# Hybrid decoder trunk in float32: one split of a weight block for both halves of the sequence, with the second half's products parked in DRAM

## The chip, the cores and the metric

The kernel runs on one core of a Trainium2 chip. The metric is device time in microseconds: the median of the runs shown, and beside it one profiled execution with its trace. In the views, PE is TensorE (matrix products), PEld its weight loads, DVE is VectorE, ACT is ScalarE, POOL is GpSimd and SP is SyncE, from whose queue most transfers are issued.

## The reference

Two layers act on a sequence of 1024 rows of width 1024, in float32. Layer 0 is the hybrid mixer; the change lies in its input projection. Cut to that part:

```python
proj = x @ w_in
qa, ka, va, qkv_b, z, beta_logit, a_logit = split_cols(proj, HYB_SPLITS)
o_a = sliding_window_attention(rope(qa), rope(ka), va, sinks)        # 8 heads of 64, window 128
qkv_b = silu(causal_dwconv(qkv_b, conv_w))                           # width 4, over rows
qb, kb, vb = split_cols(qkv_b, (B_W, B_W, B_W))                      # 4 heads of 128
o_b = gated_delta_rule(l2_normalize(qb), l2_normalize(kb), vb, g, beta)
o_b = rms_norm(o_b) * norm_w * silu(z)
mix = concatenate([o_a, o_b]) @ w_out
x = layer_norm(alpha * x + mix)
x = layer_norm(alpha * x + sqrelu_mlp(x))                            # 1024 -> 4096 -> 1024
```

Layer 1 has a gated linear recurrence in the mixer's place, and the same MLP.

## The kernel before

**Two chunks.** The sequence is cut into two chunks of 512 rows, `c` = 0 and 1. Each is a Python generator, `stream(c)`: hybrid mixer, output projection and layer norm (`mix_out`), MLP and layer norm (`mlp_ln`), then the same for layer 1. Chunk 1 needs from chunk 0 the last three rows of each convolution (`halo`), the delta states (`Sst`) and the previous keys and values of the attention.

**Products.** Every float32 operand of a large product is split in two parts of a shorter format, `h` (a cast) and `l` (the rest, by subtraction). `mm3` makes one product from three matmuls (h x h, h x l, l x h). `wblock` loads a weight block of 128x1024 into `ws` (three buffers), and `split` casts it into `wh` on ACT (each fifth one on VectorE) and subtracts into `wl` on VectorE or GpSimd (two buffers each). `proj_fm` projects a block of 128 output features: 8 steps of `mm3`, 24 matmuls of 128x512, into one PSUM bank of the four called `mm`. The four banks called `mx` take the small products. All matmuls are issued at line 206, transposes at line 210, and all other instructions at line 178, a wrapper.

**The hybrid stage.** `hybrid(c)` makes k, v and the two logits (`kv_proj`, 4 blocks of 264 columns), the queries of the attention (`q_proj`, 4 blocks), and per delta head four blocks by `proj_fm`: k, q, v in `head_front` (convolution, then silu into a tile of a ring) and z in `head_z`. `head_mid` is a head's scan: a chain of small products on PE with VectorE and ACT between, its last part four steps over the state `S`. Chunk 0 takes its tiles from two rings by turns, `t` (11 tiles, heads 0 and 2) and `s` (10 tiles, heads 1 and 3), and so has two scans under way; chunk 1 has `t` alone and one scan. A scan holds 8 tiles of its ring, of which three come from `head_front`. The ring `f` (4 tiles) holds rows for convolutions and for z. A ring's tile is asked for with `need(ring, n)`, which blocks the generator until n are free. Large tiles `g` (14) hold activations: a chunk's x takes four.

**What sets the order.** PE's order is written by the program: a main loop steps the generators, and a planner (`Clock`) keeps an estimate of every engine's time. Scans, attention, layer norms and loads of x run as `mixers`, which go first whenever the planner thinks their inputs ready; otherwise the loop takes the next step of a stream, streams in an earlier `phase` first, chunk 0 before chunk 1. A stream that is blocked gives way to the other. The order on the other queues, SP among them, is set by the framework's scheduler from the dependencies.

**The MLP.** `mlp` works in groups of 512 hidden features. `straight` makes a group with 4 + 4 blocks. `seven` makes a pair of groups' second product with seven block products in place of eight; it uses sums of weight blocks that are built in DRAM (`t1` to `t4`, loads `ws<-t`). Chunk 0 goes over from `straight` to pairs at an even group, once chunk 1's output projection is done (`"op"`) and two `g` tiles are free.

Of the kernel before, what the change touches and what calls it, by code (L numbers as in the profile page):

```python
# [9 lines left out]
F32 = mybir.dt.float32  # L10
# [7 lines left out]
P = 128  # L18
D = 1024
T = 1024  # L20
CH = 512
NT = CH // P
KT = D // P
# [190 lines left out]
def trunk(ctx: ExitStack, tc, I, out):  # L214
    nc = tc.nc
    clk = Clock(tc, nc)
    V, G, S, PE = clk.engine(nc.vector, "V"), clk.engine(nc.gpsimd, "G"), clk.engine(nc.scalar, "S"), clk
    DS, DA, DG = clk.engine(nc.sync, "V"), clk.engine(nc.scalar, "V"), clk.engine(nc.gpsimd, "V")
# [9 lines left out]
    dpool = ctx.enter_context(tc.tile_pool(name="dpool", bufs=1, space=bass.MemoryType.DRAM))  # L228
# [23 lines left out]
    def tl(r, dt=F32):  # L252
        return take(r, tpool.tile([P, FW if r == "f" else 512], dt, tag=r, name=nm(r), bufs=RINGS[r]))

    def ts(r, dt=F32):
        return tl(r, dt)[:, :512]

    def free(r, *tiles):
        rings[r] += len(tiles)
        spare[r] += [t.name for t in tiles]  # L260
        assert rings[r] <= (GB if r == "g" else RINGS[r])

    def need(r, n=1):
        return wait(lambda: rings[r] >= n)
# [4 lines left out]
    def wait(cond):  # L269
        while not cond():  # L270
            yield BLOCK
# [77 lines left out]
    def wblock(src, n=1024, hl=None, pool=True):  # L349
        st = clk.tile("ws", WS, wpool.tile([P, 1024], F32, tag="ws", name=nm("ws"), bufs=WS))[:, :n]  # L350
        DS.dma_start(st if len(src.shape) == 2 else st.rearrange("p (q c) -> p q c", q=2), src)
        if hl is None:
            hl = [clk.tile(t, WB, wpool.tile([P, 1024], F32R, tag=t, name=nm(t), bufs=WB))[:, :n] for t in ("wh", "wl")]
        h, l = hl
        split(h, l, st, pool and wcount[0] % LG)
        m = n // 2
        return [h[:, :m], h[:, m:]], [l[:, :m], l[:, m:]]

    def mm3(ps, lh, ll, rh, rl, start, stop, more=False):

        PE.matmul(ps, lh, rh, start=start, stop=False, fresh=more)
        PE.matmul(ps, lh, rl, start=False, stop=False, fresh=more)
        PE.matmul(ps, ll, rh, start=False, stop=stop, fresh=more)
# [34 lines left out]
    def load_xT(c, x, k2):  # L398
        if c == 0:
            st = [ts("t") for _ in range(2)]  # L400
            for j in range(2):
                DS.dma_start(st[j], I["xT"][:, 2 * k2 + j, :CH])
            free("t", *st)
        else:
            st = clk.tile("ws", WS, wpool.tile([P, 1024], F32, tag="ws", name=nm("ws"), bufs=WS))[:, :1024]
            DS.dma_start(st.rearrange("p (k t) -> p k t", k=2), I["xT"][:, 2 * k2:2 * k2 + 2, CH:])
            st = [st[:, :512], st[:, 512:]]
        for j in range(2):
            k = 2 * k2 + j
            S.copy(x.h(k), st[j])  # L410
            V.tensor_tensor(x.l(k), st[j], x.h(k), ALU.subtract)

    def proj_fm(src, x, bank=None, pool=True):
        wh, wl = wblock(src, pool=pool)
        ps = (bank or mm_ps)()
        for k in range(KT):
            b, c = divmod(k, 4)
            mm3(ps, wh[b][:, c * P:(c + 1) * P], wl[b][:, c * P:(c + 1) * P], x.h(k), x.l(k), k == 0, k == KT - 1)
            if k < KT - 1:
                yield  # L420
        return ps

    def proj_tm(srcs, x, n, nk=KT, pre=None, pool=True):
        ps = [mm_ps() for _ in range(NT)]
# [335 lines left out]
    def q_proj(c, x, st, oT):  # L760
        ps = yield from proj_tm([I["hin_q"][i] for i in range(4)], x, 512)
        st["q"] = [oT.quad(0, n) for n in range(NT)]
        for n in range(NT):
            split_ps(*st["q"][n], v4(ps[n]))
        yield UNIT
# [140 lines left out]
    def conv4(raw, y, tmp, wt, bias=None, pool=True):  # L906
        if bias is None:
            S.activation(y, raw[:, 0:512], AF.Copy, scale=wt(0))
        else:
            S.activation(y, raw[:, 0:512], AF.Identity, bias=bias, scale=wt(0))  # L910
        S.activation(tmp, raw[:, 1:513], AF.Copy, scale=wt(1))
        (G if pool else V).tensor_tensor(y, y, tmp, ALU.add)
        for j in range(2, 4):
            V.scalar_tensor_tensor(y, raw[:, j:j + 512], wt(j), y, ALU.mult, ALU.add)

    def head_front(c, h, x, d, r):
        for j, name in enumerate("kqv"):
            yield from need(r, 1)
            yield from need("f", 2)
            raw, y, u = tl("f"), ts("f"), ts(r)  # L920
            ps = yield from proj_fm(I["hin_fm"][h * 4 + j], x)
            i = h * 3 + j
            if c == 0:
                G.memset(raw[:, 0:3], 0.0)
            else:
                G.tensor_copy(raw[:, 0:3], halo[:, i, :])
            S.copy(raw[:, 3:515], ps)
            if c == 0:
                G.tensor_copy(halo[:, i, :], raw[:, 512:515])
            conv4(raw, y, u, lambda k: W["hcw"][:, i * 4 + k:i * 4 + k + 1])  # L930
            S.activation(u, y, AF.Tanh, scale=0.5)
            V.scalar_tensor_tensor(u, u, 1.0, y, ALU.add, ALU.mult)
            free("f", raw, y)
            d[name] = u
            yield UNIT

    def head_z(h, x, oT, d):
        yield from need("f")
        z = ts("f")
        ps = yield from proj_fm(I["hin_fm"][h * 4 + 3], x)  # L940
        S.activation(z, ps, AF.Tanh, scale=0.5)
        V.scalar_tensor_tensor(z, z, 1.0, ps, ALU.add, ALU.mult)
        S.copy(oT.h(4 + h), z)
        V.tensor_tensor(oT.l(4 + h), z, oT.h(4 + h), ALU.subtract)
        free("f", z)
        d["z"] = True
        yield UNIT

# [265 lines left out]
    def spawn(g, t=0.0):  # L1214
        mixers.append([lambda: t, g])

    def slots(n):
        slot["g"] = [gran() for _ in range(n // 4)]
        return [g[:, i * 512:(i + 1) * 512] for g in slot["g"] for i in range(4)]
# [20 lines left out]
    def load_x(c, x):  # L1240
        yield from need("g", 4)
        x.claim()
        for k2 in range(KT // 2):
            load_xT(c, x, k2)
            t = clk.now + 7.0
            yield lambda: t
        st[c]["x"] = True

    def hybrid(c, x, oT, st, rs):
        d = [dict() for _ in range(4)]  # L1250
        if c == 0:
            slot["tl"] = slots(8)
            yield from kv_proj(c, x, st, oT, lambda k2: load_xT(c, x, k2))
            DS.dma_start(csb, I["consts"])
        else:
            yield from wait(lambda: "x" in st)
            yield from head_front(c, 0, x, d[0], rs[0])
            yield from wait(lambda: sts[0].get("att", 0) >= 2)
            yield from kv_proj(c, x, st, oT, None)
        spawn(delta_scalars(c, st))  # L1260

        def q():
            yield from need("g", 2)
            yield from q_proj(c, x, st, oT)
            o = [dict() for _ in range(NT)]
            spawn(attention(c, st, oT, o))
            spawn(attn_preps(c, st, o))
        par = len(rs) > 1
        if not par:
            yield from q()  # L1270
        for h in range(4):
            if h or par:
                yield from head_front(c, h, x, d[h], rs[h % len(rs)])
            if not par and h:
                if h == 1:
                    yield from wait(lambda: "ln0" in sts[0])
                    yield from need("g", 2)
                yield from head_z(h - 1, x, oT, d[h - 1])
            yield from wait(lambda: h - st.get("scan", 0) < len(rs))
            spawn(head_mid(c, h, st, d[h], oT, rs[h % len(rs)]))  # L1280
            if h == 1 and par:
                yield from q()
                yield from need("g", 2)
                yield from head_z(0, x, oT, d[0])
                yield from head_z(1, x, oT, d[1])
                spawn(load_x(1, xTs[1]))
        if par:
            yield from head_z(2, x, oT, d[2])
        yield from head_z(3, x, oT, d[3])
        x.free()  # L1290
        yield from wait(lambda: st.get("mids") == 4 and st.get("att") == 4)

    def mix_out(w, oT, resid, which, r, s, t, hold):
# [34 lines left out]
    sts = st  # L1328

    xTs = [ActT(), ActT()]  # L1330
# [30 lines left out]
    while streams or mixers:  # L1361
        m = next((m for m in mixers if m[0]() + MARGIN <= clk.now), None) if clk.bank("mx", 4) <= clk.now else None
        if m is not None:
            r = next(m[1], "end")
# [11 lines left out]
        for c in ([cur] if cur is not None else sorted(streams, key=lambda c: (c == shy, phase[c], c))):  # L1376
            r = next(streams[c], "end")
# [129 lines left out]
```

## Time and profile before

| what | value |
|---|---|
| median of 3 runs | 2313.34 us (2312.12 to 2314.28) |
| profiled execution, its own time | 2313.61 us |
| its span, first to last instruction | 2311.8 us |
| PE busy | 2226.8 us, 96% of the span |
| VectorE, ACT, GpSimd busy | 1552.7, 1026.1, 313.6 us |
| loads of 512 KB of `hin_fm` (the blocks of `proj_fm` in the hybrid stage) | 32 |
| loads of 512 KB of sums for `seven` | 88 |
| mean granted clock of PE | 0.988 |

The profile's page gives busy time per engine, the span in 40 slices, the DMA queues, the chain of work that ended last and the costliest groups of instructions. A group's row has the line, the engine, the operation, output<-inputs, shapes and count; then busy time, mean nanoseconds of one, and the idle time of the engine just before with what ended it. A busy PE is not always a fast one: matmuls are pipelined, and the clock that it is granted is a column of its own.

### The profile page before, as it was taken

Reading aid. Unit: us, or ns where it says so; the run is one execution under the profiler, and the core shown is the slowest. Engines: PE = TensorE matmul, PEld = TensorE weight load, DVE = VectorE, ACT = ScalarE, POOL = GpSimd, SP = SyncE. Lnnn points to the kernel's source line nnn. Section 1 sums busy time; section 2 is a strip of 40 time slices with the busy share of each in tenths; the row PEclk is TensorE's granted clock in tenths of the full one; section 3 lists DMA queues with packets and bytes.
Section 4 is the critical chain, followed back from the end, with each engine's and each line's share of the span. In section 5 each row is a group of like instructions: output and inputs, shape, how many; then the busy total and the mean of one; then the engine's idle time right before and its main releaser. Section 6 shows DMA issues by size and latency. Waiting matters only on the chain.

```text
span 2311.8 us, 32057 instructions
## 1 busy us (share of the span) xinstructions
PE 2226.8 (96%) x12460; PEld 1795.1 (78%) x12460; DVE 1552.7 (67%) x2706; ACT 1026.1 (44%) x1759; POOL 313.6 (14%) x248
## 2 busy tenths in 40 slices
PE   8999997999999999999999999989999999999997
PEld 7676776667777888788888878868888887888886
DVE  6788759456645463686666898675565566776477
ACT  5364424433433233454444677474424434444442
POOL 3433223223322120000000001021100000000100
PEclk9999998999999999999999999999999999999999
DMA  4221232556667656677744335222523443454341
GB/s 159 65 74 36 75 123 74 146 153 180 178 177 231 193 162 187 191 237 232 222 139 155 119 129 170 93 74 96 182 95 127 138 146 125 156 166 137 128 159 69
DMA packets 86200, 329.08 MB, mean 142 GB/s; under 512 B 9504, under 2 KB 9888, under 8 KB 77856
## 3 DMA queue, kind: packets, MB, share of 16 engines
q1 hardware_dynamic: 72944, 272.17, 34.4%
q0 software_dynamic: 4608, 33.56, 7.6%
q10 hardware_dynamic: 8496, 21.30, 2.7%
q8 instruction: 98, 1.61, 0.3%
q14 instruction: 54, 0.44, 0.1%
HBM read 318.60 MB, written 75.50 MB: 170 GB/s over the span
## 4 chain that ended last, share of the span: by engine, by line
PE 78%; DVE 13%; ACT 3%; issue 2%; POOL 0%; DMA 0%; DVEq 0%; ACTq 0%; POOLq 0%
PE mm L206 61%; PE mx L206 16%; DVE g L178 5%; DVE t L178 2%; DVE s L178 2%; DVE hsc L178 2%; DVE wl L178 1%; PE mx L210 1%; DVE f L178 1%; ACT wh L178 1%; ACT g L178 1%; ACT t L178 1%; ACT s L178 1%; ACT f L178 0%; ACT L178 0%
## 5 line engine op out<-in xcount | busy, mean ns | idle before, releaser
L206 PE MATMUL mm<-g,wh 128*128 128x512 f32 x2816 | 890.1, 397 | 2.7 <-DVE g L178 2.6
L178 DVE TENSOR_TENSOR wl<-ws,wh 128x1024 fp32r<-128x1024 f32 (+1 forms) x374 | 456.8, 1222 | 340.0 <-ACT wh L178 336.7
L178 ACT CAST wh<-ws 128x1024 fp32r<-128x1024 f32 (+1 forms) x350 | 365.1, 1043 | 719.9 <-PE mm L206 620.6
L206 PEld LDWEIGHTS mm<-g,wh 128*128 128x128 f32 x2816 | 522.2, 189 | 111.3 <-DVE g L178 3.9
L206 PE MATMUL mm<-g,wl 128*128 128x512 f32 x1408 | 551.8, 392 | 0.0
L206 PE MATMUL mm<-wh,s 128*128 128x512 f32 x1152 | 379.8, 395 | 3.6 <-DVE g L178 3.3
L206 PEld LDWEIGHTS mm<-g,wl 128*128 128x128 f32 x1408 | 266.0, 189 | 57.0
L178 POOL TENSOR_TENSOR wl<-ws,wh 128x1024 fp32r<-128x1024 f32 (+1 forms) x64 | 157.2, 2457 | 1010.1 <-ACT wh L178 861.4
L206 PEld LDWEIGHTS mm<-wh,s 128*128 128x128 f32 x1152 | 216.2, 188 | 51.1 <-DVE g L178 3.9
L206 PE MATMUL mm<-wh,g 128*128 128x512 f32 (+1 forms) x768 | 231.4, 379 | 9.3 <-ACT wh L178 6.4
L206 PE MATMUL mm<-wl,s 128*128 128x512 f32 x576 | 224.6, 390 | 0.0
L206 PE MATMUL mx<-wh,s 128*128 128x512 f32 x528 | 172.7, 392 | 1.8 <-DVE s L178 1.8
L206 PEld LDWEIGHTS mm<-wh,g 128*128 128x128 f32 x768 | 142.3, 190 | 35.9 <-ACT wh L178 6.4
L206 PE MATMUL mm<-wl,g 128*128 128x512 f32 (+1 forms) x384 | 143.8, 375 | 0.3 <-DVE wl L178 0.3
L178 ACT CAST s<-g 128x512 fp32r<-128x512 f32 x158 | 96.4, 623 | 100.3 <-PE mm L206 51.2
L178 DVE TENSOR_TENSOR s<-g,s 128x512 fp32r<-128x512 f32 x158 | 106.8, 687 | 38.7 <-ACT s L178 38.5
L206 PEld LDWEIGHTS mm<-wl,s 128*128 128x128 f32 x576 | 108.3, 188 | 20.6 <-DVE wl L178 0.3
L206 PEld LDWEIGHTS mx<-wh,s 128*128 128x128 f32 x528 | 99.1, 188 | 23.2 <-DVE s L178 3.1
L178 DVE CAST wh<-ws 128x1024 fp32r<-128x1024 f32 x88 | 62.7, 712 | 78.1 <-PE mm L206 68.4
L178 DVE TENSOR_TENSOR g<-g,mm 128x512 f32<-128x512 f32 x144 | 95.0, 683 | 20.0 <-PE mm L206 19.5
L206 PE MATMUL mx<-wl,s 128*128 128x512 f32 x264 | 102.8, 389 | 0.0
L206 PEld LDWEIGHTS mm<-wl,g 128*128 128x128 f32 x384 | 73.2, 191 | 12.2 <-DVE wl L178 0.6
(241 smaller groups left out, 2703.2 us busy)
## 6 DMA issues: line engine op xcount, KB each, us to landing
ws<-w SPq DMA_DIRECT2D x234, 512.0 KB, 3.3
ws<-t SPq DMA_DIRECT2D x88, 512.0 KB, 3.3
t<-w POOLq DMA_DIRECT2D x32, 1024.0 KB, 8.6
ws<-hin_fm SPq DMA_DIRECT2D x32, 512.0 KB, 3.3
t<-w SPq DMA_DIRECT2D x16, 1024.0 KB, 7.5
t<-t SPq DMA_DIRECT2D x16, 1024.0 KB, 6.5
ws<-rin SPq DMA_DIRECT2D x32, 512.0 KB, 3.3
ws<-hout SPq DMA_DIRECT2D x16, 512.0 KB, 3.3
```

What stands on the lines that cost most here:

```text
L178: r = f(*a, **k)
L206: ins = self.pe.matmul(out, lhsT, rhs, start=start, stop=stop, skip_group_check=fresh)
L210: return self._pe(self.pe.transpose(out, x, ident), out, [x], 0.00042 * 2 * out.shape[-1])
```

## The change

Chunk 0 takes over the products of 13 of chunk 1's 16 blocks: k, q, v of heads 1, 2, 3 and z of all four heads. `proj_fm` gets a second activation (`also`) and a second PSUM bank, and makes the three matmuls of a step for one chunk and then for the other from the same split block. The second result is copied by ACT into a ring tile and stored to DRAM (`park`, from SP). Chunk 1 loads it from SP straight into the tile that the copy from PSUM used to fill. Head 0 of chunk 1 is projected as before.

For this, chunk 1's x is loaded and split from the end of chunk 0's `kv_proj` on, where before it followed the second z; head 1 of chunk 0 waits for it. Chunk 0's `q_proj` moves from behind head 1 to behind head 0. `head_front` asks for two ring tiles in place of one for a shared block, and `head_z` for two `f` tiles in place of one. Chunk 1's x is freed after the later of chunk 0's last z and chunk 1's q.

```diff
-    def proj_fm(src, x, bank=None, pool=True):
+    def proj_fm(src, x, bank=None, pool=True, also=None):
         wh, wl = wblock(src, pool=pool)
-        ps = (bank or mm_ps)()
+        xs = [x] if also is None else [x, also]
+        ps = [(bank or mm_ps)() for _ in xs]
         for k in range(KT):
             b, c = divmod(k, 4)
-            mm3(ps, wh[b][:, c * P:(c + 1) * P], wl[b][:, c * P:(c + 1) * P], x.h(k), x.l(k), k == 0, k == KT - 1)
-            if k < KT - 1:
-                yield
-        return ps
+            for i, z in enumerate(xs):
+                mm3(ps[i], wh[b][:, c * P:(c + 1) * P], wl[b][:, c * P:(c + 1) * P], z.h(k), z.l(k), k == 0, k == KT - 1)
+                if k < KT - 1 or z is not xs[-1]:
+                    yield
+        return ps[0] if also is None else ps
...
+    parked = {}
+
+    def park(i, ps, o):
+        parked[i] = dpool.tile([P, CH], F32, name=f"parked_{i}", tag=f"parked_{i}")
+        S.copy(o, ps)
+        DS.dma_start(parked[i], o)
+
-    def head_front(c, h, x, d, r):
+    def head_front(c, h, x, d, r, also=None):
         for j, name in enumerate("kqv"):
-            yield from need(r, 1)
+            i = h * 3 + j
+            yield from need(r, 1 + (also is not None))
             yield from need("f", 2)
             raw, y, u = tl("f"), ts("f"), ts(r)
-            ps = yield from proj_fm(I["hin_fm"][h * 4 + j], x)
-            i = h * 3 + j
+            if c and i in parked:
+                DS.dma_start(raw[:, 3:515], parked[i])
+            else:
+                ps = yield from proj_fm(I["hin_fm"][h * 4 + j], x, also=also)
+                if also is not None:
+                    o = ts(r)
+                    park(i, ps[1], o)
+                    free(r, o)
+                    ps = ps[0]
...
-            S.copy(raw[:, 3:515], ps)
+            if not (c and i in parked):
+                S.copy(raw[:, 3:515], ps)
...
-    def head_z(h, x, oT, d):
-        yield from need("f")
-        z = ts("f")
-        ps = yield from proj_fm(I["hin_fm"][h * 4 + 3], x)
+    def head_z(c, h, x, oT, d, also=None):
+        yield from need("f", 2)
+        z, o = ts("f"), ts("f")
+        if c and 12 + h in parked:
+            ps = o
+            DS.dma_start(ps, parked[12 + h])
+        else:
+            ps = yield from proj_fm(I["hin_fm"][h * 4 + 3], x, also=also)
+            if also is not None:
+                park(12 + h, ps[1], o)
+                ps = ps[0]
...
     def hybrid(c, x, oT, st, rs):
         if c == 0:
...
+            spawn(load_x(1, xTs[1]))
...
         par = len(rs) > 1
+        both = xTs[1] if par else None
         if not par:
             yield from q()
+            drop()
         for h in range(4):
+            if h and par:
+                yield from wait(lambda: "x" in sts[1])
             if h or par:
-                yield from head_front(c, h, x, d[h], rs[h % len(rs)])
+                yield from head_front(c, h, x, d[h], rs[h % len(rs)], both if h else None)
...
             spawn(head_mid(c, h, st, d[h], oT, rs[h % len(rs)]))
+            if h == 0 and par:
+                yield from q()
             if h == 1 and par:
-                yield from q()
                 yield from need("g", 2)
-                yield from head_z(0, x, oT, d[0])
-                yield from head_z(1, x, oT, d[1])
-                spawn(load_x(1, xTs[1]))
+                yield from head_z(c, 0, x, oT, d[0], both)
+                yield from head_z(c, 1, x, oT, d[1], both)
         if par:
-            yield from head_z(2, x, oT, d[2])
-        yield from head_z(3, x, oT, d[3])
-        x.free()
+            yield from head_z(c, 2, x, oT, d[2], both)
+        yield from head_z(c, 3, x, oT, d[3], both)
+        if par:
+            x.free()
+            drop()
```

More of the change, by code (lines that the diff above doesn't have):

```diff
@@ L944, in head_z @@
         V.tensor_tensor(oT.l(4 + h), z, oT.h(4 + h), ALU.subtract)
-        free("f", z)
+        free("f", z, o)
         d["z"] = True
@@ L1247, in load_x, with drop @@
         st[c]["x"] = True
+    users = [0, 1]
+    def drop():
+        if not users.pop():
+            xTs[1].free()
     def hybrid(c, x, oT, st, rs):
@@ L1277, in hybrid @@
                     yield from need("g", 2)
-                yield from head_z(h - 1, x, oT, d[h - 1])
+                yield from head_z(c, h - 1, x, oT, d[h - 1])
             yield from wait(lambda: h - st.get("scan", 0) < len(rs))
             spawn(head_mid(c, h, st, d[h], oT, rs[h % len(rs)]))
+            if h == 0 and par:
+                yield from q()
             if h == 1 and par:
-                yield from q()
                 yield from need("g", 2)
-                yield from head_z(0, x, oT, d[0])
-                yield from head_z(1, x, oT, d[1])
-                spawn(load_x(1, xTs[1]))
+                yield from head_z(c, 0, x, oT, d[0], both)
+                yield from head_z(c, 1, x, oT, d[1], both)
         if par:
-            yield from head_z(2, x, oT, d[2])
-        yield from head_z(3, x, oT, d[3])
-        x.free()
+            yield from head_z(c, 2, x, oT, d[2], both)
[3 more added lines that the diff above has]
+            drop()
         yield from wait(lambda: st.get("mids") == 4 and st.get("att") == 4)
```

## The prediction

> **What bounds the kernel now.** I read the page first (busy shares, the clock row, the chain that ended last), then the table of stretches over the first layer's hybrid stage, then what PE waited for there, then VectorE's groups in the worst stretch.
>
> ```profile
> PE 2226.8 (96%) x12460; PEld 1795.1 (78%) x12460; DVE 1552.7 (67%) x2706; ACT 1026.1 (44%) x1759; POOL 313.6 (14%) x248
> PE   8999997999999999999999999989999999999997
> DVE  6788759456645463686666898675565566776477
> PEclk9999998999999999999999999999999999999999
> PE 78%; DVE 13%; ACT 3%; issue 2%; POOL 0%; DMA 0%; DVEq 0%; ACTq 0%; POOLq 0%
> L178 DVE TENSOR_TENSOR wl<-ws,wh 128x1024 fp32r<-128x1024 f32 (+1 forms) x374 | 456.8, 1222 | 340.0 <-ACT wh L178 336.7
> L178 ACT CAST wh<-ws 128x1024 fp32r<-128x1024 f32 (+1 forms) x350 | 365.1, 1043 | 719.9 <-PE mm L206 620.6
> L178 POOL TENSOR_TENSOR wl<-ws,wh 128x1024 fp32r<-128x1024 f32 (+1 forms) x64 | 157.2, 2457 | 1010.1 <-ACT wh L178 861.4
> ```
>
> PE is busy 96% and makes 78% of the chain, so a split that is left out (1.04 us on ACT, 1.22 on VectorE or 2.46 on GpSimd) is worth nothing by itself: it lies beside matmuls. The change moves no matmul count either. What it can win is PE's idle time, so the question is in which stretch that lies. In the next view the columns are stretch, length, busy time of PE, PEld, DVE, ACT, POOL, granted clock, DMA share and GB/s.
>
> ```profile
> 60.00:97.00 37.00, 33.26 (x573) 25.66 (x574) 25.91 (x64) 10.30 (x31) 12.74 (x11) 1.00 0.23 72
> 97.00:190.00 93.00, 84.45 (x579) 63.63 (x578) 82.25 (x203) 50.88 (x145) 37.10 (x35) 0.96 0.21 69
> 190.00:263.00 73.00, 68.37 (x893) 45.81 (x892) 53.22 (x146) 30.59 (x86) 16.24 (x14) 0.95 0.12 33
> 263.00:305.00 42.00, 39.38 (x252) 35.13 (x251) 31.24 (x84) 16.77 (x48) 13.17 (x9) 1.00 0.31 101
> 305.00:354.00 49.00, 46.04 (x201) 37.23 (x200) 26.28 (x36) 8.57 (x10) 8.70 (x6) 1.00 0.41 140
> 354.00:400.00 46.00, 33.80 (x243) 26.73 (x241) 45.42 (x126) 27.70 (x68) 15.80 (x12) 0.86 0.18 66
> 400.00:783.00 383.00, 373.28 (x2814) 284.29 (x2814) 216.63 (x480) 144.49 (x330) 103.88 (x72) 0.99 0.63 178
> 783.00:1240.00 457.00, 455.37 (x2021) 375.60 (x2020) 289.64 (x397) 188.38 (x256) 21.74 (x17) 1.00 0.62 192
> 1200.00:1250.00 50.00, 50.00 (x222) 41.40 (x221) 28.74 (x33) 19.42 (x25) 0.00 (x0) 1.00 0.44 148
> ```
>
> By the order of the weight loads, 60 to 305 us is the first chunk's heads, attention and delta scans (with the second chunk's first head, its k/v and most of its q between), 305 to 354 the first chunk's output projection, 354 to 400 its layer norm, 400 to 783 its MLP with the second chunk's remaining heads inside. Idle of PE: 3.7 + 8.6 + 4.6 + 2.6 = 19.5 us up to 305; 12.2 us in the layer norm; 9.7 us in the MLP stretch; 1.6 in the 457 us after it. Half clock costs 0.04 x 93 + 0.05 x 73 = 7.4 us more up to 305. A gapless stretch gives 50 / 222 = 0.225 us for one 512-column matmul, so one weight block (8 x 3 = 24 of them) is 5.4 us of PE.
>
> What PE waits for up to 305, and the longest wait of the layer norm:
>
> ```profile
> PE mx L206 <- DVE S L178: 5.3, 3, 3.0
> PE mx L206 <- DVE s L178: 4.1, 3, 2.6
> ...
> PE mx L206 <- DVE t L178: 7.0, 1, 7.0
> ```
>
> All on the `mx` products of scan and attention, for VectorE; none for a weight block.
>
> **The change part by part, with its cost.**
>
> Moved matmuls. 13 blocks (k, q, v of heads 1 to 3, four z) are multiplied with both halves of the sequence in the first chunk: 13 x 5.4 = 70.3 us of PE come into the stretch that ends at 305. The second chunk loses 3 of these blocks (head 1) from the layer-norm gap, 16.2 us, and 10 (heads 2 and 3, four z) from the MLP stretch, 54.1 us.
>
> What the first stretch absorbs. Its idle and half-clock time is 27 us, the upper bound; the lower bound is 0, since the same `mx` steps still wait in order on VectorE. VectorE's own work there stays (25.9 + 82.3 + 53.2 + 31.2 = 192.6 us of 245, 79%), but would spread over some 300 us (64%), so waits should fall, not vanish: I take 14, the middle. The stretch grows by 70.3 - 14 = 56.3.
>
> The MLP stretch. PE is busy 97% of it, filled by the first chunk's own matmuls, so the 54.1 us come off in full; of its 9.7 us idle I take 2 more, since ten blocks' splits and their casts leave VectorE and ACT. Bounds 0 and 9.7.
>
> The layer-norm gap. Here PE is idle and VectorE is busy 45.42 of 46 us: VectorE sets its length. Its groups there:
>
> ```profile
> L178 DVE TENSOR_TENSOR g<-g,s 128x512 f32<-128x512 f32 x14 | 12.2, 909 | 0.0
> L178 DVE SCALAR_TENSOR_TENSOR f<-f,sm,f 128x512 f32<-128x512 f32 x5 | 4.1, 813 | 0.0
> L178 DVE TENSOR_TENSOR g<-g,asc 128x512 f32<-128x512 f32 x3 | 3.8, 1324 | 0.0
> L178 DVE CUSTOM_DVE_ANT_0 g<-mx,csb 128x256 f32<-128x256 f32 x8 | 3.0, 413 | 0.0
> L178 DVE TENSOR_TENSOR wl<-ws,wh 128x1024 fp32r<-128x1024 f32 x2 | 2.4, 1196 | 0.0
> ```
>
> The norm's own work (first row) stays. Two splits go (2.4 us); head 1's convolutions (4.1) and the second chunk's first attention block (3.8 + 3.0) can slide ahead of the gap, because the second chunk's first head, k/v and q now run while the first chunk finishes its longer stretch. That is 13.3; bounds 0 (they stay) and 16.2 (the gap shrinks by all the matmuls it loses). I take 8.
>
> Parking. Added: 13 copies of a 128x512 bank on ACT, 13 stores and 13 loads of 256 KB on SP. Removed: 13 loads of 512 KB with their casts, and nine copies of the second chunk. Rows for these: the copy, the load, a 256 KB store and a 256 KB load.
>
> ```profile
> L178 ACT COPY f<-mm x40: 562/579/590, 27.3 to 1609.5; 128x512 f32<-128x512 f32 x40
> ws<-hin_fm SPq DMA_DIRECT2D x32, 512.0 KB, 3.3
> out<-g SPq DMA_DIRECT2D x16, 256.0 KB, 2.0
> t<-ln ACTq DMA_DIRECT2D x24, 256.0 KB, 4.8
> ```
>
> ACT: 13 x 0.58 = 7.5 us spread over a stretch where it is busy 28 to 55%, and every shared block has 10.8 us of matmuls over it: hidden; without that cover 7.5. The load of a parked half (2.0 to 4.8 us) replaces 5.4 us of matmuls at the head of a convolution: not later than before. On SP a store waits for its copy, and the weight loads queued behind it wait too. Against that: the stores of the output, which wait for VectorE in the same way, go out between weight loads without holding them.
>
> ```profile
> 2003.07 1.08 SPq L178 DMA_DIRECT2D out<-g  x2
> 2004.93 0.33 SPq L178 DMA_DIRECT2D ws<-t  x1
> ```
>
> Bounds 0 and 13 x (3.3 + 1.04 + 1.22) = 72 us if each store exposed the next load and split; nearest row says 0, I take 1. The second half's x is loaded and split some 50 us earlier: same work, in a stretch where PE has work; 0.
>
> Sum: +70.3 - 14 - 54.1 - 2 - 8 + 1 = -6.8 us. The profiled execution took 2313.61 (span 2311.8), 0.27 above the median of 2313.34; so 2306.5.
>
> **Rivals.**
>
> (A, slower) The first chunk's delta chain, not PE, sets the end of the longer stretch. Rows: head 1's last block is copied at 59.88, the last state update of heads 0 and 1 is at 166.06, head 3's last block at 186.99, the last update of all at 290.20.
>
> ```profile
> 59.88 0.57 ACT L178 COPY f<-mm 128x512 f32<-128x512 f32 x1
> 166.06 0.33 DVE L178 SCALAR_TENSOR_TENSOR S<-S,dsc,mx 128x128 f32<-128x128 f32 x1
> 186.99 0.57 ACT L178 COPY f<-mm 128x512 f32<-128x512 f32 x1
> 290.20 0.34 DVE L178 SCALAR_TENSOR_TENSOR S<-S,dsc,mx 128x128 f32<-128x128 f32 x1
> ```
>
> Now q (4 blocks, 21.6 us) and head 1's second halves (16.2) come ahead of head 1's scan: it ends near 166 + 38 = 204. Head 3 shares head 1's ring of 10 tiles and asks for two free ones per block, so its q and v wait for that. From 97 to 263 a block of 5.4 us took 166 / 13 = 12.8 us beside the `mx` steps; two double blocks take 30 to 51 us, head 3 is complete at 234 to 255 instead of 187, and the stretch ends 47 to 68 us later. Up to 56 PE is the bound and nothing is lost; from there every microsecond is. At 68: -6.8 + 12 = +5.2, 2318.5; with the gap unchanged too, 2326.5.
>
> (B, no change) The gap keeps its 46 us without the 16.2 us of matmuls in it: 2314.5. For it: VectorE full; against it: its load moves ahead. The clock bears on it: in a part of the gap where PE was busy 3.01 of 6.80 us, the granted clock was 0.50.
>
> ```profile
> 383.90:390.70 6.80, 3.01 (x38) 2.49 (x39) 6.80 (x16) 4.54 (x17) 1.58 (x3) 0.50 0.00 0
> ```
>
> An emptier gap could stay at half clock past its end; a stretch like this one costs 3.4 us, which gives 2318. The Trainium skill ("TensorE: Matmul & The Clock Gate", What's actually happening) states such a gate: half rate after about 3.4 us without enough PE work, full rate after as long of it; the row agrees.
>
> (C, no change) The first chunk's MLP has one pair of groups by seven products, taken only if the second chunk's output projection is done at an even group; it was, at group 6: that projection's last load is at 801.40 and the first load of a sum at 925.57.
>
> ```profile
> 801.40 0.33 SPq L178 DMA_DIRECT2D ws<-hout  x1
> 925.57 0.33 SPq L178 DMA_DIRECT2D ws<-t  x1
> ```
>
> The MLP now gets 54.1 us more of PE before that point, more than one group's 8 blocks (43 us). If it enters group 6 first, the pair goes straight: 24 matmuls more, +5.4, 2312. If the second chunk's heads run faster by as much, nothing changes.
>
> (D, much faster) All 27 us are absorbed and the gap shrinks by 16.2: -13 - 8.2 more, 2285. For it: VectorE's share falls in both; against it: waits on `mx` steps stay in order.
>
> **How the numbers follow.** About 0.2% (4.6 us) is what a measurement tells from no change. Forecast 0.35 and D 0.17 are faster, 0.52; B 0.12 and C 0.10 within, 0.22; A 0.22 and the SP queue 0.04 slower, 0.26. The range is 2285 (D) to 2327 (A with B). The likeliest case's own range, from bounds nearer the middle (absorbed 10 to 20, gap 5 to 12), is 2296 to 2313.
>
> **What would show it.** Loads of `hin_fm` fall from 32 to 19; 13 stores and 13 loads of parked tiles; the first chunk's layer norm starts 50 to 60 us later than at 354; the layer norm's stretch is under 46 us; the first chunk's MLP reaches its 925 us mark earlier by some 7 us; loads of `ws<-t` stay 88 (80 is C). A stretch of PE idle just ahead of the first `hout` matmuls is A. Wrong would be: PE waits on `wh` or `wl` while SP holds a parked store, or an MLP stretch that loses fewer than 54 us.

## The result, and the profile after

The changed kernel takes 2339.81 us (median of 4 runs, 2337.04 to 2343.46) against 2313.30 (2312.12 to 2314.28): a ratio of 1.0116, 95% interval 1.0098 to 1.0133. It is 26.5 us slower; 2306.5 was forecast. The profiled execution took 2340.8 us, its span is 2338.9.

The page of the changed kernel: busy shares, slices, the chain that ended last, and the splits.

```profile
PE 2238.2 (96%) x12460; PEld 1801.8 (77%) x12460; DVE 1532.8 (66%) x2699; ACT 1016.9 (43%) x1753; POOL 284.8 (12%) x239
PE   8999999599989999999999999989999999999997
DVE  6664656858474455677666899686564566786477
PEclk9999999799999999999999999999999999999999
PE 82%; DVE 12%; ACT 3%; issue 2%; DMA 1%; POOL 1%; POOLq 0%; SPq 0%; DVEq 0%; ACTq 0%
L178 DVE TENSOR_TENSOR wl<-ws,wh 128x1024 fp32r<-128x1024 f32 (+1 forms) x370 | 453.5, 1226 | 331.4 <-ACT wh L178 327.5
L178 ACT CAST wh<-ws 128x1024 fp32r<-128x1024 f32 (+1 forms) x341 | 355.3, 1042 | 641.8 <-PE mm L206 545.9
L178 POOL TENSOR_TENSOR wl<-ws,wh 128x1024 fp32r<-128x1024 f32 (+1 forms) x55 | 130.7, 2376 | 909.1 <-DVE wh L178 496.2
```

PE issues the same 12460 matmuls and shows the same 96%. Thirteen splits are gone (4 on VectorE, 9 on GpSimd), and the time is longer. The hole in PE's row has moved and grown deeper: before it is the seventh slice, with PE at 7 and its clock at 8; now it is the eighth (409 to 468 us), with PE at 5 and its clock at 7. The share of busy time doesn't tell the two kernels apart; the table of stretches does (stretch, length, busy time of PE, PEld, DVE, ACT, POOL, granted clock, DMA share, GB/s):

```profile
60.00:97.00 37.00, 33.30 (x403) 25.17 (x403) 21.92 (x61) 11.72 (x31) 12.40 (x12) 0.95 0.14 49
97.00:375.00 278.00, 270.35 (x2224) 207.01 (x2224) 169.79 (x438) 108.89 (x296) 71.29 (x65) 0.99 0.17 57
375.00:424.00 49.00, 47.15 (x207) 38.12 (x206) 22.79 (x30) 9.19 (x11) 6.24 (x5) 1.00 0.43 150
424.00:480.00 56.00, 26.72 (x290) 18.02 (x288) 49.92 (x142) 24.34 (x64) 17.96 (x12) 0.70 0.21 76
480.00:852.00 372.00, 358.79 (x2667) 276.98 (x2668) 217.28 (x482) 143.52 (x330) 96.20 (x67) 0.99 0.63 177
852.00:1260.00 408.00, 402.91 (x1781) 331.69 (x1780) 263.68 (x371) 172.74 (x235) 11.52 (x14) 1.00 0.67 204
```

The first chunk's output projection ends at 424, 70 us later than at 354: the 70.3 us that were moved in came in full. The layer norm's stretch is 56 us in place of 46, with PE busy 26.72 us in place of 33.80 and the clock at 0.70 in place of 0.86. From 423.97 to 479.51 PE issues no matmul of a projection at all. Matmuls that PE could make while it waits are called cover below. What PE waits for there (columns: waited for, us in all, times, longest; "issue" is time in which it waits for nothing that the profile shows):

```profile
PE mx L210 <- DVE f L178: 9.9, 1, 9.9
PE mx L210 <- DVE g L178: 7.2, 1, 7.2
PE mx L210 <- issue: 6.3, 1, 6.3
PE mx L206 <- DVE lnw L178: 2.9, 1, 2.9
```

These are transposes and small products of the norm and of the second chunk's first head and attention block. VectorE, busy 49.92 of 56 us, feeds them one after another, and nothing lies between them. VectorE's own order has changed too. The last add of the output projection and the norm's last scaling on VectorE, in the kernel before and in the changed kernel (start, us, engine, line, operation):

```profile
355.47 0.67 DVE L178 SCALAR_TENSOR_TENSOR g<-g,mm 128x512 f32<-128x512 f32 x1
364.22 0.74 DVE L178 SCALAR_TENSOR_TENSOR g<-g,lnw,s 128x512 f32<-128x512 f32 x1
425.20 0.67 DVE L178 SCALAR_TENSOR_TENSOR g<-g,mm 128x512 f32<-128x512 f32 x1
442.71 0.74 DVE L178 SCALAR_TENSOR_TENSOR g<-g,lnw,s 128x512 f32<-128x512 f32 x1
```

The way from the one to the other is 8.8 us before and 17.5 in the changed kernel, where four operations of the second chunk's convolutions (`f<-f,sm,f`) and eight of its attention block (`g<-mx,csb`) lie in between; before, none does. The counts of transfers are as forecast:

```profile
ws<-t SPq DMA_DIRECT2D x88, 512.0 KB, 3.6
ws<-hin_fm SPq DMA_DIRECT2D x19, 512.0 KB, 3.3
f<-parked SPq DMA_DIRECT2D x13, 256.0 KB, 2.7
parked<-s SPq DMA_DIRECT2D x6, 256.0 KB, 2.0
parked<-f SPq DMA_DIRECT2D x4, 256.0 KB, 2.9
parked<-t SPq DMA_DIRECT2D x3, 256.0 KB, 2.3
```

**A measure for the comparisons.** For every matmul take the time from its start to the next one's start, less the usual time of its shape (the 30th percentile of that shape in the trace before), and sum: PE's loss, with waits, half clock and pipeline breaks in it. It is worked out from the records of the traces, not a view. Span less loss is 2146 to 2147 us in every kernel with 88 loads of `ws<-t`, 2141 with 96, 2152 with 80, 2159 with 72: a pair of groups that goes straight costs 24 matmuls, 5 to 7 us, and all else is loss. Three stages: to 24 us after the last load for chunk 0's output projection; from there (layer norm, MLP) to the first load for chunk 1's; the rest.

| kernel | `ws<-t` | first | norm, MLP | rest | loss | span |
|---|---|---|---|---|---|---|
| before | 88 | 66.6 | 69.0 | 29.4 | 165.0 | 2311.8 |
| changed | 88 | 65.6 | 91.7 | 35.3 | 192.6 | 2338.9 |
| nothing in DRAM | 88 | 63.9 | 93.2 | 31.3 | 188.3 | 2335.7 |
| changed, q put back | 88 | 68.2 | 93.3 | 32.5 | 194.0 | 2340.7 |
| early x alone | 88 | 76.2 | 68.8 | 29.1 | 174.1 | 2320.7 |
| ten blocks | 80 | 65.8 | 72.7 | 35.2 | 173.7 | 2325.7 |
| ten, x beside q | 80 | 66.9 | 73.1 | 35.2 | 175.2 | 2327.0 |
| eight, order of before | 80 | 71.9 | 76.1 | 45.0 | 193.0 | 2344.9 |
| q held back | 72 | 68.8 | 70.8 | 38.8 | 178.4 | 2337.2 |
| q held back, pair kept | 88 | 73.9 | 70.6 | 38.5 | 183.0 | 2330.0 |
| ten, x by `s` | 80 | 63.8 | 75.7 | 35.5 | 175.0 | 2327.0 |
| ten, x by `s`, pair kept | 88 | 67.8 | 74.7 | 29.3 | 171.8 | 2319.0 |

Changed against before: -1.0, +22.7, +5.9 us; the sum is 27.6, the spans differ by 27.1. Of the -1.0, the first 100 us lose 8.3 more and the rest of the stage 9.3 less. Of the +22.7, the norm's stretch has 19.6 (21.6 from 354 to 400 us before, 41.2 from 424 to 480 now).

The same by the marks of the two traces: the norm's stretch starts 70 us later (354 and 424), it is 10 us longer, from its end to the first load of a sum (925.57 and 946.55) it is 59.0 us less, and behind that 6.1 more. Together that is 27.1.

### The profile page after: what moved, and what is told of

Its sections match the earlier page's. It is cut to its first block, busy times and chain, and to the rows that moved or that the text cites. A ratio compares the mean times of both kernels' runs of the same rounds, so it can differ in the third digit from the quotient of the medians.

```text
span 2338.9 us, 32057 instructions
## 1 busy us (share of the span) xinstructions
PE 2238.2 (96%) x12460; PEld 1801.8 (77%) x12460; DVE 1532.8 (66%) x2699; ACT 1016.9 (43%) x1753; POOL 284.8 (12%) x239
## 4 chain that ended last, share of the span: by engine, by line
PE 82%; DVE 12%; ACT 3%; issue 2%; DMA 1%; POOL 1%; POOLq 0%; SPq 0%; DVEq 0%; ACTq 0%
PE mm L206 63%; PE mx L206 17%; DVE g L178 5%; PE mx L210 2%; DVE wl L178 1%; ACT g L178 1%; DVE hsc L178 1%; DVE s L178 1%; DVE f L178 1%; DVE t L178 1%; DMA ws<-w 1%; ACT wh L178 1%; ACT s L178 0%; DVE lnw L178 0%; DMA f<-parked 0%
## 5 line engine op out<-in xcount | busy, mean ns | idle before, releaser
L178 ACT CAST wh<-ws 128x1024 fp32r<-128x1024 f32 (+1 forms) x341 | 355.3, 1042 | 641.8 <-PE mm L206 545.9
L206 PE MATMUL mm<-wh,s 128*128 128x512 f32 x1216 | 405.1, 398 | 9.7 <-DVE g L178 9.3
L206 PEld LDWEIGHTS mm<-wh,s 128*128 128x128 f32 x1216 | 230.5, 190 | 62.7 <-DVE g L178 12.1
L206 PE MATMUL mm<-wl,s 128*128 128x512 f32 x608 | 239.0, 393 | 2.8 <-DVE wl L178 2.8
L178 POOL TENSOR_TENSOR wl<-ws,wh 128x1024 fp32r<-128x1024 f32 (+1 forms) x55 | 130.7, 2376 | 909.1 <-DVE wh L178 496.2
L206 PEld LDWEIGHTS mm<-wl,s 128*128 128x128 f32 x608 | 115.5, 190 | 25.6 <-DVE wl L178 3.6
L178 DVE CAST wh<-ws 128x1024 fp32r<-128x1024 f32 x84 | 57.8, 688 | 83.2 <-PE mm L206 69.2
L178 ACT ACTIVATE g<-mm 128x512 f32<-128x512 f32 x92 | 54.5, 593 | 71.7 <-PE mm L206 71.7
```

What stands on the lines that cost most here:

```text
L178: r = f(*a, **k)
L206: ins = self.pe.matmul(out, lhsT, rhs, start=start, stop=stop, skip_group_check=fresh)
```

## The experiments

Edits are shown against the changed kernel. Ratios are to the kernel before, run on the same chip (2312.29 to 2314.19 us).

**1. The order alone, without sharing.**

```diff
-        both = xTs[1] if par else None
+        both = None
```

(x and `f` tiles freed as before.)

> No block is shared; only the order is the change's: chunk 1's x is loaded right after chunk 0's k/v projection, chunk 0's q projection comes ahead of head 1, head 1 waits for chunk 1's x. Theory (lost cover: the moved matmuls find no idle time in the first stretch and leave the layer-norm gap empty): no matmul is moved, so 2310 to 2322, and the gap after chunk 0's output projection keeps head 1's three blocks and stays near 45 us. Rival (order: the delay of head 1's scan by q and the early load of x cost the time): 2330 or more.

2332.22 us, ratio 1.0082 (1.0067 to 1.0097): the order costs 18.7 us with nothing shared, as the rival had it, and at that with 96 loads of `ws<-t`, 5 to 6 us less of matmuls. PE's loss is 188.9 us, 23.9 over the kernel before and only 3.7 under the changed kernel. A lost cover that needs the sharing can't be all. (By stages this kernel can't be set beside the others: blocks of the second chunk's heads lie inside its first chunk's output projection. It too has a hole without a matmul of a projection, of 25.5 us from 444.74 on.)

**2. Head 1 not shared, the other ten blocks shared.**

```diff
-                yield from head_front(c, h, x, d[h], rs[h % len(rs)], both if h else None)
+                yield from head_front(c, h, x, d[h], rs[h % len(rs)], both if h > 1 else None)
```

> As the changed kernel, but head 1 is not shared: ten blocks (heads 2 and 3, four z) are moved, and chunk 1 projects its head 1 itself in the layer-norm gap. Theory (lost cover): the ten blocks cost 54 us in the first stretch and save 54 us in the MLP stretch, the gap keeps its 16 us of matmuls, so 2308 to 2322. Rival (parking: DRAM round trips, the SP queue, more ring tiles cost the time): ten of thirteen parked blocks remain, so about 10/13 of the 26 us, 2333. Rival (order): 2330 or more.

2330.8 us, ratio 1.0075 (1.006 to 1.009), with one pair straight: above my range, in that of the order and near that of parking. Still, the loss in norm and MLP is 72.7 us in place of 91.7, and the first stage doesn't move: head 1's three blocks alone make 19 us of difference. The norm's stretch of this kernel:

```profile
408.00:460.00 52.00, 39.20 (x290) 29.81 (x290) 49.90 (x135) 29.77 (x71) 16.48 (x13) 0.87 0.30 104
```

and PE's longest waits in it:

```profile
PE mx L206 <- DVE t L178: 7.1, 1, 7.1
PE mm L206 <- ACT g L178: 1.5, 1, 1.5
```

VectorE is as busy as in the changed kernel (49.90), PE has 12.5 us more to do beside it, the clock is 0.87, and of the long waits one of 7.1 is left, as before (7.0). But VectorE's order is that of the kernel before as well: from the last add to the norm's last scaling it takes 8.7 us. The run brings back both at once, the cover and VectorE's order.

**3. Head 1 shared alone.**

```diff
-                yield from head_front(c, h, x, d[h], rs[h % len(rs)], both if h else None)
+                yield from head_front(c, h, x, d[h], rs[h % len(rs)], both if h == 1 else None)
```

(z unshared too.)

> Only head 1's three blocks are shared and parked. Theory (lost cover): 16 us of matmuls move from the layer-norm gap, where they cost nothing, to the first stretch, where they cost their time: 2326 to 2340, with a gap without large matmuls. Rival (parking): three of thirteen, about +6: 2320. Rival (order): 2330 or more, told apart by the run without sharing.

2348.72 us, ratio 1.0153 (1.0137 to 1.017): 16.5 us over the order alone, and above the range of every theory. There are two stretches without a matmul of a projection, of 38 us just ahead of the output projection and of 37 us behind it:

```profile
327.00:365.00 38.00, 16.81 (x184) 13.52 (x182) 37.16 (x105) 15.60 (x54) 17.56 (x15) 0.63 0.25 90
446.00:483.00 37.00, 17.67 (x91) 10.04 (x89) 28.73 (x93) 15.62 (x36) 4.99 (x4) 0.68 0.28 71
```

**4. Nothing in DRAM.** No store; two ACT copies of a standing table in place of each load.

```diff
-        DS.dma_start(parked[i], o)
...
-                DS.dma_start(raw[:, 3:515], parked[i])
+                for m in (3, 259):
+                    S.copy(raw[:, m:m + 256], stand)
```

> As the changed kernel, but nothing goes through DRAM: the parked results are not stored, and where chunk 1 would load them two ACT copies of a 128x256 table in SBUF fill the tile, so chunk 1's heads 1 to 3 and its z are left out of the result. Theory (lost cover): the transfers are hidden, 2334 to 2344. Rival (parking: late loads, SP queue held by stores): most of the 26 us goes, 2313 to 2322.

2337.23 us, ratio 1.0104 (1.0089 to 1.0119), 2.6 us under the changed kernel with the intervals overlapping. The norm's stretch has the same hole (58 us, PE busy 28.15, clock 0.71). The traffic with DRAM isn't the cause; the copies and the tiles of parking are still there.

**5 to 7. The order's two parts.** The changed kernel with q put back behind head 1; without sharing, the early x alone; without sharing, q's move alone. The edit of the first:

```diff
-            if h == 0 and par:
-                yield from q()
             if h == 1 and par:
+                yield from q()
```

> The changed kernel with chunk 0's q projection put back behind head 1's front end; all thirteen blocks stay shared and chunk 1's x stays early. Two theories of the order's cost (+18.7 us where the order alone was changed). Theory q: q ahead of head 1 makes head 1's scan late (its state updates began at 211 us in the changed kernel, 132 before), so that chunk 0's delta work and the layer norm behind it end later: putting q back takes 15 to 22 us off the changed kernel's 2339.8, to 2318 to 2325, with head 1's lost cover still in it. Theory x: it is the early load of chunk 1's x (its transposes and splits in the first stretch, and the wait for them) that costs; then this kernel stays at 2336 to 2342.

2340.82 us, ratio 1.012 (1.0104 to 1.0135).

> Nothing shared; of the order only the early load of chunk 1's x and head 1's wait for it are kept, q is behind head 1 as in the kernel before. Theory q: 2311 to 2317. Theory x: 2328 to 2334, as with the whole order.

2322.55 us, ratio 1.0048 (1.0029 to 1.0067).

> Nothing shared; of the order only q's place ahead of head 1 is kept, chunk 1's x is loaded behind z1 as in the kernel before. Theory q: 2328 to 2334. Theory x: 2311 to 2317. If both parts cost some, e6 and this one lie between and their excesses add up to about 19 us.

2313.93 us, ratio 1.0005 (0.9996 to 1.0014), with 96 loads of `ws<-t`; its loss is 171.1.

The theory that q's place is the cost falls: put back in the changed kernel it returns nothing, and alone it leaves the time as it is. That isn't quite nothing: its loss is 6.1 us over the kernel before, and the one pair more by seven products hides them. The early x costs 10.3 us, less than theory x had. The two together cost more than their sum (18.7; by the loss 23.9 against 9.1 and 6.1); why isn't settled. What goes on in the stretch where the early x costs, on SP's queue and in the engines, early x alone:

```profile
15.07 0.34 SPq L178 DMA_DIRECT2D ws<-hin_fm  x1
17.88 0.38 SPq L178 DMA_DIRECT2D ws<-xT  x1
19.88 0.33 SPq L178 DMA_DIRECT2D ws<-hin_fm  x1
23.51 1.67 SPq L178 DMA_DIRECT2D ws<-xT  x2
27.39 4.57 SPq L178 DMA_DIRECT2D ws<-hin_fm  x3
```

```profile
20.00:45.00 25.00, 18.49 (x75) 14.83 (x74) 15.12 (x33) 13.56 (x32) 8.46 (x8) 0.86 0.59 184
```

and the kernel before in the same 25 us:

```profile
20.00:45.00 25.00, 24.40 (x119) 19.94 (x119) 13.14 (x33) 13.93 (x46) 13.21 (x13) 1.00 0.35 117
```

Transfers of x stand between the weight blocks of heads 0 and 1; PE issues 75 matmuls in place of 119, at a clock of 0.86. That the transfers are the reason is not shown. PE's longest waits from 20 to 100 us, early x alone, are all for VectorE and none for a weight block:

```profile
PE mx L210 <- DVE t L178: 7.2, 2, 5.2
PE mx L206 <- DVE dsc L178: 5.4, 1, 5.4
```

In the kernel before the longest there is 2.2 us. VectorE has the subtractions of chunk 1's x to make in this stretch, and which of the two, transfers or subtractions, holds PE up wasn't tried by itself.

"q put back" and "early x alone" have the same order and differ in the sharing (with the tiles that it asks for): the cleanest pair. Sharing takes 8.0 us off the loss of the first stage, adds 24.5 to norm and MLP, 3.4 to the rest: +19.9, the spans differ by 20.0. Their first stages from 100 us on, early x alone and then q put back:

```profile
100.00:357.00 257.00, 243.15 (x2093) 186.29 (x2092) 191.07 (x465) 104.95 (x282) 79.85 (x67) 0.99 0.22 70
100.00:420.00 320.00, 312.96 (x2404) 241.05 (x2403) 194.49 (x492) 121.06 (x321) 83.21 (x73) 0.99 0.21 71
```

PE's idle time falls from 13.9 to 7.0 us: the added matmuls do fill waits. But +19.9 is the price of sharing on top of this order. On top of the whole order ("the order alone", 188.9) it is 3.7. So the 27.6 us don't come apart in one way into order and sharing; what the traces fix is where they lie in the changed kernel.

**8. Ten blocks, q behind head 1, x loaded beside q.**

```diff
+            if h == 1 and par:
+                spawn(load_x(1, xTs[1]))
+                yield from q()
+                yield from wait(lambda: "x" in sts[1])
```

(no early load; head 1 unshared.)

> Ten blocks shared (heads 2 and 3 and the four z), not head 1's; q behind head 1 as before, and chunk 1's x loaded beside q, waited for ahead of z0. If the three losses are the order (+18.7), head 1's cover (+9 to +16) and little else, and the ten blocks gain some 12 us at equal numbers of matmuls, this kernel comes to 2298 to 2308, faster than both. The rival, that a longer first stretch costs whatever its order (the delta chain of chunk 0 sets its end), gives 2313 to 2325.

2328.74 us, ratio 1.0068 (1.0053 to 1.0084): above both ranges. The gain of 12 us that I had given to the ten blocks was a comparison across kernels whose order differed; the loss of the first stage is 66.9, that of the kernel before.

**9. Eight blocks, order of before.** Heads 2, 3 and their z, x loaded behind z1.

```diff
-            if h and par:
+            if h == 2 and par:
                 yield from wait(lambda: "x" in sts[1])
```

(q and the load of x where they were, no sharing of head 1, z0, z1.)

> The order of the kernel before throughout (q behind head 1, chunk 1's x loaded behind z1), with the eight blocks shared that still come after that load: k, q, v of heads 2 and 3 and z of these two. Theory one: the early load of chunk 1's x costs about 10 us of PE in the first 100 us, and the shared blocks give about as much back by filling PE's waits behind the scans' small products, so that the two cancel in every kernel with an early x; without the early load the first stretch loses 6 to 8 us less and the kernel comes to 2306 to 2313 (5.4 more if one pair of groups of the first MLP goes straight, with 80 loads of sums). Theory two: the shared blocks fill nothing, the waits stay as they are: 2313 to 2322, 5.4 more with a straight pair.

2346.39 us, ratio 1.0137 (1.012 to 1.0154): outside both. Without an early load, the program has head 2 wait for x, and from 118.45 to 143.36 us PE issues no matmul of a projection. About there it runs dry:

```profile
130.00:160.00 30.00, 20.76 (x77) 16.28 (x77) 14.21 (x47) 5.44 (x17) 2.55 (x2) 0.72 0.09 32
```

PE's waits in these 30 us are for small tiles of VectorE and ACT (`s`, `t`, `S`), the longest 3.8 us; that the wait for x is the reason is not shown. The first stage loses 71.9, and the later ones more than in other kernels (76.1, 45.0), which no run here explains.

**10. The changed kernel, chunk 1's q held back into the gap.**

```diff
         if not par:
+            yield from wait(lambda: "op" in sts[0])
             yield from q()
```

> The changed kernel, with chunk 1's q projection (4 blocks, 13 to 16 us of matmuls in 256-column pieces) held back until chunk 0's output projection is done, so that it lies in the gap of chunk 0's layer norm. Theory cover: the gap of 55 us costs because nothing is left to put into it: the kernel falls by 10 to 16 us, to 2324 to 2330. Theory chain: chunk 0's scans (last state update at 360 us) set the end of the first stretch, and PE idles there for what it gave away: 2336 to 2344.

2341.39 us, ratio 1.0121 (1.0106 to 1.0136), as the theory of the chain had it, but not for its reason. The loss in norm and MLP falls from 91.7 to 70.8, as the cover had it; the first stage loses 3.2 more; and two pairs more go straight (72 loads, 48 matmuls, some 12 us). (The q projection is 96 matmuls of 512 columns, so 21.6 us of cover and not 13 to 16.) Ahead of the output projection, and in the norm:

```profile
345.00:365.00 20.00, 12.33 (x70) 10.69 (x69) 12.98 (x49) 6.95 (x27) 3.57 (x4) 0.74 0.34 106
405.00:472.00 67.00, 52.23 (x294) 42.73 (x293) 59.48 (x139) 29.69 (x59) 25.49 (x17) 0.86 0.46 145
```

With q gone, PE idles 7.7 us ahead of the output projection. Its longest wait there, 6.0 us, is for `dsc`, a small tile that VectorE makes from the second chunk's logits; the last state update of the first chunk's scans is at 353.04, in the middle of this stretch. From the last add to the norm's last scaling VectorE takes 6.8 us: here too the cover comes together with another order on VectorE.

**11 to 13.** Ten blocks, with chunk 1's x loaded through tiles of ring `s`; the same, with chunk 0's MLP waiting for `"op"` after its sixth group; and number 10 with that wait.

```diff
-            st = clk.tile("ws", WS, wpool.tile([P, 1024], F32, tag="ws", name=nm("ws"), bufs=WS))[:, :1024]
+            st = [ts("s") for _ in range(2)]
...
             yield from straight(e, e == 7)
+            if c == 0 and e == 5:
+                yield from wait(lambda: sts[1].get("op", -1) >= layer and rings["g"] >= 2)
```

> The kernel with ten blocks shared (not head 1's, 2330.8), with chunk 1's x loaded through tiles of the ring s, idle then, in place of the weight buffers ws: eight transfers of 256 KB in place of four of 512 KB, with no weight buffer taken. Theory buffers: the early x delays the weight blocks behind it in the three ws buffers, and PE ran dry for it at 30 to 40 us: 5 to 10 us less, 2321 to 2326. Theory bandwidth: what delays the blocks is the bytes themselves, at a time when the transfers run at over 200 GB/s: within 2 us of 2331.

2333.08 us, ratio 1.0089 (1.0072 to 1.0106): not the weight buffers. The first stage loses 2 us less than with ten blocks (number 2), no more.

> The same as e11_x_by_s, and chunk 0's MLP waits after its sixth group until chunk 1's output projection is done, so that its last two groups go as a pair by seven products (88 loads of sums, as in the kernel before). Theory: the number of matmuls explains 24 x 0.225 = 5.4 us of the loss, and PE has chunk 1's output projection to do while chunk 0 waits: 5 to 6 us under e11. Rival: chunk 0's MLP is the cover of chunk 1's last scan, and the wait opens an idle stretch of as much or more: not under e11.

2322.94 us, ratio 1.0043 (1.0028 to 1.0058), the best of the kernels with sharing: 10.1 us under number 11 (8.0 by the spans), more than the 5.4 of matmuls: the loss in the rest falls too, from 35.5 to 29.3, and that of the first stage is 4.0 higher. The rows of PE, without and with the wait:

```profile
PE 2238.9 (96%) x12484; PEld 1801.0 (77%) x12484; DVE 1514.7 (65%) x2676; ACT 1011.4 (43%) x1744; POOL 325.2 (14%) x251
PE 2232.6 (96%) x12460; PEld 1794.5 (77%) x12460; DVE 1534.9 (66%) x2699; ACT 1019.9 (44%) x1755; POOL 300.7 (13%) x243
```

> The kernel with chunk 1's q held back into the gap (2341.4), with the same wait after the sixth group, which brings the matmuls of large tiles back to the number of the kernel before (it had two straight groups' worth more, 48 matmuls). Theory: holding q gave back the lost cover of the gap, some 14 to 20 us of PE, and straight groups hid 10.8 of it: 2328 to 2332 here. Rival: the cover is worth nothing and the extra matmuls filled idle time of PE: within 3 us of 2341.

2334.05 us, ratio 1.0089 (1.0074 to 1.0104): 2 us over the range, 7.3 under number 10 and 5.8 under the changed kernel. Holding q is worth 21 us in norm and MLP, as number 10 had shown; 8.3 go to the first stage and 3.2 to the rest.

No version with sharing beat the kernel before.

## Why the prediction was wrong, step by step

**What bounds the kernel.** Right: PE; and that a split left out is worth nothing by itself. The matmuls' sum never moved, and each time follows from PE's loss and the number of pairs.

**Moved matmuls, +70.3 and -54.1.** Right: 69.8 more up to the end of the output projection, and 59.0 less from the end of the norm's stretch to the first load of a sum. That load comes 21 us later all the same, not 7 earlier, since the norm starts 70 us later and takes 10 us longer.

**What the first stretch absorbs, -14.** This failed in the sum, not in the mechanism: sharing fills 8.0 us of waits ("q put back" against "early x alone"), within the bounds of 0 and 27. The term was 6 us too large.

**The second half's x earlier, 0.** This step failed: "same work, in a stretch where PE has work" took it for granted that PE would go on. It costs 9.6 us of loss in the first stage ("early x alone"); whether by the transfers among the weight blocks or by VectorE's subtractions stays open. Moving q gives 2.6 back, so absorption and early x nearly cancel: -1.0 in place of -14.

**The layer-norm gap, -8, and the MLP stretch, -2.** This step failed most: +22.7 of loss in place of -10. 19.6 of it lie in the norm's stretch, 3.0 in the MLP. The gap got longer, 56 us, not shorter. The second chunk's convolutions and attention block did not slide ahead of it (VectorE is busy 49.92 us, 45.42 before) but into the norm's own chain on VectorE, which takes 17.5 us in place of 8.8; and the cover went. The chain takes 17.5 to 19.6 us in the three kernels that share all thirteen blocks and don't hold q ("changed", "nothing in DRAM", "q put back"), and 6.8 to 8.8 in all the others of the table. Leaving head 1 unshared or holding q brings back the cover and the short chain together, so the runs show that head 1's blocks are worth 19.0 there and not how much of this each of the two is. Rival B named the lost cover and priced it at 8 for the missing gain (3.5 more for the clock); 19.0 is more than the 16.2 us of matmuls that lay in the gap. The clock is part of it: in the gap's worst part

```profile
440.00:470.70 30.70, 8.76 (x59) 5.48 (x59) 28.85 (x70) 12.23 (x29) 11.33 (x8) 0.50 0.20 71
```

PE is at half clock for 30.7 us, with PE busy 29%; the prediction had shown a part of 6.8 us, and the longest in the trace before is 10.2 (397.6 to 407.8). The Trainium skill ("TensorE: Matmul & The Clock Gate", What's actually happening) has the clock fall after a window of some 3.4 us without enough work. The trace agrees, 30.7 being nine such windows.

**Parking, +1.** About right: the traffic with DRAM is worth 2.6 us, not told apart from nothing. The copies weren't taken out.

**The rest, not in the sum.** +5.9 us of loss behind the first MLP had no term. Part of it goes without the DRAM traffic (31.3 in place of 35.3); the remainder is open.

**Rivals.** A's price was for an end of the first stretch set by the scans. Its mark, idle PE ahead of the `hout` matmuls, isn't there (270.35 of 278 us busy from 97 to 375), though 7.7 us of it come up once q is held back, and with head 1 shared alone PE is busy just 16.81 of the 38 us ahead of that projection. C didn't occur in the changed kernel (88) but did in five of the thirteen others, and is worth 10.1 (number 11 against 12) with the loss that goes with it. D had no ground: 8.0 us were absorbed, and the gap grew.

## What to carry to other kernels

Where TensorE is the bound and its matmuls stay the same, sharing a split can only win idle time, so the work that leaves a stretch must be priced as the cover that it was there: three blocks taken out of the layer norm cost 19 us, more than twice the 8 that thirteen shared blocks gave back elsewhere. Work that gets free of its matmuls comes earlier on the other engines too: look whose chain it lands in. An operand needed earlier brings its transfers and its splits into a stretch that others use: price both there. And where the schedule decides by timing how many matmuls are made (here the pairs of groups), read that count ahead of any time: each 24 matmuls are 5 to 7 us here, and 48 of them hid more than half of a gain of 21 in one run.

## What the runs showed of the hardware, unexpected

The gap in which VectorE sets the pace was longer with matmuls taken out of it: 46 us with PE busy 33.80 and the clock at 0.86, 56 with 26.72 and 0.70. Of the 10 us, 4.5 are VectorE's busy time and the rest its idle time. The norm's chain on VectorE, with the second chunk's work in it, is 8.8 us longer. That the halved clock of the small products lengthens VectorE's waits may have a part in it; neither was tried by itself. The load of a parked half was not always in time: ACT waited 6.7 us in two places of the second chunk for it, its row in the list of what ended ACT's idle time ahead of `f` (490 to 860 us):

```profile
  DMA f<-parked: 6.7, 2
```
